# A dense product-key expert layer: 48 instead of 32 tokens of the last tile taken out of the dense stage, with rearranged PSUM, selection and tail

## The chip, the cores and the metric

The kernel runs on one core of one Trainium2 chip. The core has five engines with an instruction queue each: TensorE (PE in the profile, its weight loads PEld), VectorE (DVE), ScalarE (ACT), GpSimd (POOL) and SyncE (SP, which only issues DMAs here). They wait for each other by semaphores. The metric is the device time of one execution in microseconds (us), the median of several runs; smaller is better.

## The reference, cut to what matters

Two decoder layers over 512 tokens of width 1024. Each is a mixer (gated linear attention in the first, stick-breaking attention in the second, both with memory attention), a residual with layer norm, and then a PEER layer: every token picks 8 x 16 of 16384 experts, and each expert is one row of a table `u` and one row of a table `v`.

```python
def peer(x, w_q, subkeys, u_tab, v_tab):
    ...
    q = (xf @ w_q).reshape(N, PEER_HEADS, 2, PEER_QHALF)
    s = jnp.einsum('nhpd,hpkd->nhpk', q, subkeys).astype(jnp.float32)
    top_s, top_i = lax.top_k(s, PEER_TOPK)
    ...
    best_s, best_pos = lax.top_k(cand_s, PEER_TOPK)
    idx = jnp.take_along_axis(cand_i, best_pos, axis=-1)
    g = jax.nn.softmax(best_s, axis=-1).astype(x.dtype)
    ...
        act = jax.nn.gelu(jnp.einsum('nd,nhkd->nhk', xt, u_tab[it]), approximate=False)
        return jnp.einsum('nhk,nhkd->nd', gt * act, v_tab[it])
```

All data are 32-bit. The products run as three matmuls on a split of both operands into a high and a low part (`hi*hi`, `hi*lo`, `lo*hi`).

## The kernel before

The 512 tokens are four tiles of 128. All four are treated alike up to the selection of experts; then the work of `peer` (line 1122 on) is divided in three ways.

- **Tile 0 is gathered.** For each of its 128 (head, k) places one indirect DMA from POOL fetches 128 rows of `u` (512 KB, tile `gr`), and DVE multiplies them with x and sums up (`gather_u`, tile `gh`); later the same is done with rows of `v`, added up with weights in `va` (`gather_v`).
- **Tiles 1 to 3 are dense**: the hidden values of all 16384 experts are computed in 128 blocks of 128 experts. A block (`ublock`) loads a block of `u` (SP, `ur`), splits it (`uh` on ACT, `ul` = `ur` - `uh` on DVE or POOL), makes 24 matmuls into a PSUM tile `ph` (8 chunks of the width by 3 products, lines 118 to 120), and ACT applies the Gelu and writes the result out to memory (`act`, tensor `Ad`; the last 16 blocks stay in SBUF as `keep`).
- **Side tokens**: the last `SD` = 32 of tile 3 are left out of these matmuls, so that a matmul moves `TU` = 384 - 32 = 352 columns. Their hidden values come from gathered rows of `u`, 16 tokens in a group: 8 heads x 16 tokens fill the 128 partitions, and 16 gathers make a group. Indices, weights and results change their layout by small trips through memory (`Si`, `Sg`, `Sw`), issued by SP. Their x stands in an SBUF tile `xr`, copied eight times by eight DMAs of SP (`side_x`, line 1170).

The gate of each dense or side token at each expert is spread out by one-hot matmuls (`pg`: two per dense token in `gate_mm`, three per side token in `side_mm`), evicted by ACT and written to memory (`Gd`, 24 groups of 16 tokens). Then follows the v stage, 128 blocks again: `vprep` loads a block of `v` (`vr`) and of the activations (`al`) and gates (`gl`), multiplies the two (`w`), splits both (`vh`, `vl`, `whi`, `wlo`), and 18 matmuls of 512 columns (`mov_mm`, lines 290 to 294) add into six PSUM tiles `acc`. The last `TAIL` = 6 blocks are held back and run tile by tile at the end, so that one tile's layer norm (`finish`) can run beside the next tile's matmuls.

The order on PE, DVE, ACT and POOL is written out by hand (`manual_schedule`). In the u stage each block has a place for other work: a small planner (constants `BLK`, `GU`, `GUA`, `GUM` and so on) gives every block a number of nanoseconds for gathers, selection and gates. `later` holds splits `ul` that have not been given to an engine; `topk16` gives one to POOL whole, a gather of tile 0 gives half to DVE and half to POOL, and `flush` gives what is left to DVE. The selection of three tiles is made while their queries are computed, the fourth's during the u stage.

PSUM has eight banks of 512 columns. During the u stage six of them rotate under one tag `ps`, for `ph`, `pg` and the small transposes alike, and two hold x of tile 0 (`xs`).

Of the kernel before, what the change touches and what calls it, by code (L numbers as in the profile page):

```python
# [64 lines left out]
@contextmanager  # L65
def psum_pool(E, **tags):

    with E.tc.tile_pool(name="ps", bufs=1, space=bass.MemoryType.PSUM, reuse_waits="tile") as p:
        E.ps, old = (p, tags), getattr(E, "ps", None)
        yield  # L70
        E.ps = old


def psum(E, name="ps", tag="ps"):
    p, tags = E.ps
    if tag == "xs":
# [923 lines left out]
def x_to_T(E, t, tag="ps"):  # L1000

    nc = E.nc
    both = psum(E, name="xtp", tag=tag) if tag == "xs" else None
    for g in range(2):
        ps = both[:, g * 512:(g + 1) * 512] if tag == "xs" else psum(E, name="xtp", tag=tag)
# [64 lines left out]
SG = 2  # L1070
SD = SG * TS
TU = TD - SD
ST = NT - 1
S0 = P - SD
NSUB = TD // TS
# [19 lines left out]
WF = 6800  # L1095
ER = 16
# [28 lines left out]
def peer(E, mixer, wq, sk, ut, vt, un, lng, lnb, out_dram=None, follow=()):  # L1125
# [11 lines left out]
    with ExitStack() as pp:  # L1137
# [74 lines left out]

        def flush():
# [3 lines left out]
        def gather_u():  # L1217
# [48 lines left out]
        def gather_v():  # L1266
# [11 lines left out]
            finish(0, [va[:, :512], va[:, 512:]])  # L1278
            yield 4000
# [4 lines left out]
        with ExitStack() as up:  # L1284
# [6 lines left out]
            def topk16(*jobs, pool=True):  # L1291

                done = later and pool
# [17 lines left out]
            class Sel:  # L1311

                def __init__(self, t):
                    self.t = t
                    self.top_s = wk.tile([P, 16, 16], F32, tag="top_s", name="top_s", bufs=3)
                    self.top_i = wk.tile([P, 16, 16], U32, tag="top_i", name="top_i", bufs=3)
# [3 lines left out]
                    self.nr = self.nc = 0  # L1320
# [13 lines left out]
                def stage2(self):  # L1334
# [5 lines left out]
                    for a, n, o, w in SEG:  # L1340
                        dst = cand[:, :, o:o + n * w].rearrange("p h (a w) -> p h a w", a=n)
                        V.tensor_add(dst, v[:, 0, :, a:a + n, None].to_broadcast([P, 4, n, w]),
                                     v[:, 1, :, None, 0:w].to_broadcast([P, 4, n, w]))
                    for q in range(0, 4, 2):
                        jobs = []
                        for k in range(q, q + 2):
                            c2 = wk.tile([P, 64], F32, tag="s2", name="c2")
# [672 lines left out]
```

## Time and profile before

| | us |
|---|---|
| runs: median (3 runs, 2811.19 to 2813.94) | 2812.4 |
| profiled execution | 2810.38 |
| its span, first to last instruction | 2808.7 |
| u stage of layer 1 and of layer 2 (first to last `ph`) | 545.5 and 545.3 |
| v stage up to its tail (layer 1 and 2) | 497.6 and 497.6 |
| DVE busy over the span | 2325.0 (83%) |
| mean DMA rate over the span | 293 GB/s |

The profile names a group of instructions by line, engine, operation and tiles (written <- read). Its windows give the busy time of each engine in a stretch, then the granted TensorE clock (1.00 is full), the mean busy share of the 16 DMA engines and the rate in GB/s. A DMA share slightly above 1 is possible, since packets overlap. A matmul's own duration is modelled; its cadence is read from the count in a stretch.

### The profile page before, as it was taken

How to read it: one execution, taken by the hardware profiler on the slowest of the kernel's cores; microseconds unless marked ns; L12 is line 12 of the kernel's file. 1: busy time of each engine (PE TensorE's matmuls, PEld its weight loads, DVE VectorE, ACT ScalarE, POOL GpSimd, SP SyncE). 2: the span in 40 equal slices, each digit the busy share in tenths (PEclk: the TensorE clock that was granted, in tenths of full speed). 3: DMA queues.
4: the chain of work that ended last, by engine and by line, in shares of the span. 5: the costliest groups of instructions: out<-in, count | busy, mean ns of one | idle time of the engine just before them, and what ended most of it. 6: DMA issues, size and time to landing. Idle time of an engine off the chain costs nothing.

```text
span 2808.7 us, 45526 instructions
## 1 busy us (share of the span) xinstructions
PE 2789.2 (99%) x16235; PEld 2476.1 (88%) x16235; DVE 2325.0 (83%) x4816; ACT 1443.0 (51%) x2701; POOL 1141.3 (41%) x839
## 2 busy tenths in 40 slices
PE   9999999999999999999999999999999999999998
PEld 8888899999999888888787889999999988888886
DVE  5565999998766898888868859999987768888888
ACT  6342458576864443434346534585868544334432
POOL 0102564665664344444100025636656733343440
PEclk9999999999999999999999999999999999999999
DMA  5332499999999999999621325999999999999994
GB/s 195 117 113 76 160 321 369 329 372 334 365 356 385 345 390 380 380 383 386 209 68 46 120 84 182 319 367 333 367 346 360 359 374 363 386 370 382 385 382 156
DMA packets 277556, 822.37 MB, mean 293 GB/s; under 512 B 36976, under 2 KB 86352, under 8 KB 270928
## 3 DMA queue, kind: packets, MB, share of 16 engines
q1 hardware_dynamic: 170336, 423.42, 41.8%
q0 software_dynamic: 83264, 303.08, 29.3%
q10 hardware_dynamic: 23728, 92.96, 8.3%
q8 instruction: 127, 2.08, 0.3%
q14 instruction: 101, 0.83, 0.1%
HBM read 723.83 MB, written 93.42 MB: 291 GB/s over the span
## 4 chain that ended last, share of the span: by engine, by line
PE 91%; DVE 6%; DMA 1%; issue 1%; ACT 0%; POOL 0%; DVEq 0%; SPq 0%; ACTq 0%; POOLq 0%
PE acc L290 12%; PE acc L294 12%; PE acc L292 12%; PE ph L118 10%; PE ph L120 10%; PE ph L119 10%; PE pq L118 2%; PE pq L119 2%; PE pq L120 2%; DVE gr L1120 1%; PE pg L1637 1%; PE pg L1638 1%; PE pss L1709 1%; PE bsp L118 1%; PE oacc L290 1%; PE oacc L294 1%
## 5 line engine op out<-in xcount | busy, mean ns | idle before, releaser
L118 PE MATMUL ph<-xhl,uh 128*128 128x352 f32 x2048 | 674.2, 329 | 0.0
L99 POOL TENSOR_TENSOR ul<-ur,uh 128x512 fp32r<-128x512 f32 (+1 forms) x222 | 382.5, 1723 | 691.3 <-DVE s L1302 366.6
L120 PE MATMUL ph<-xhl,ul 128*128 128x352 f32 x2048 | 661.0, 323 | 1.2 <-POOL ul L99 1.2
L119 PE MATMUL ph<-xhl,uh 128*128 128x352 f32 x2048 | 660.6, 323 | 0.0
L1181 POOL DMA_INDIRECT gr<-in_vt,gidx x256 | 349.1, 1364 | 482.7 <-DVE va L1274 437.9
L98 ACT ACTIVATE vh<-vr 128x1024 fp32r<-128x1024 f32 x248 | 262.7, 1059 | 431.6 <-PE acc L294 279.9
L290 PE MATMUL acc<-vh,whi 128*128 128x512 f32 x1480 | 456.1, 389 | 1.4 <-ACT whi L1863 1.4
L292 PE MATMUL acc<-vl,whi 128*128 128x512 f32 x1480 | 455.7, 389 | 0.0
L294 PE MATMUL acc<-vh,wlo 128*128 128x512 f32 x1480 | 455.7, 389 | 0.0
L98 ACT ACTIVATE uh<-ur 128x1024 fp32r<-128x1024 f32 x288 | 303.5, 1054 | 219.4 <-PE ph L119 67.0
L99 DVE TENSOR_TENSOR vl<-vr,vh 128x1024 fp32r<-128x1024 f32 x248 | 303.3, 1223 | 122.6 <-ACT vh L98 116.9
L120 PEld LDWEIGHTS ph<-xhl,ul 128*128 128x128 f32 x2048 | 385.1, 188 | 2.4 <-POOL ul L99 2.4
L119 PEld LDWEIGHTS ph<-xhl,uh 128*128 128x128 f32 x2048 | 385.7, 188 | 0.0
L118 PEld LDWEIGHTS ph<-xhl,uh 128*128 128x128 f32 x2048 | 385.4, 188 | 0.1
L1181 POOL DMA_INDIRECT gr<-in_un,gidx x256 | 298.3, 1165 | 163.7 <-DVE gr L1120 114.9
L290 PEld LDWEIGHTS acc<-vh,whi 128*128 128x128 f32 x1480 | 277.4, 188 | 60.4 <-ACT whi L1863 3.1
L292 PEld LDWEIGHTS acc<-vl,whi 128*128 128x128 f32 x1480 | 277.5, 188 | 58.2 <-DVE vl L99 0.8
L294 PEld LDWEIGHTS acc<-vh,wlo 128*128 128x128 f32 x1480 | 277.5, 188 | 58.0 <-DVE wlo L1864 0.7
L1274 DVE SCALAR_TENSOR_TENSOR va<-gr,gw,va 128x1024 f32<-128x1024 f32 x254 | 324.8, 1279 | 1.8
L1120 DVE SCALAR_TENSOR_TENSOR gr<-gr,x 128x1024 f32<-128x1024 f32 x250 | 300.4, 1213 | 0.9 <-DMA gr<-in_un,gidx 0.7
L1617 ACT ACTIVATE obl<-ob,rat 128x128 f16<-128x128 f16 x704 | 223.9, 392 | 40.8 <-DVE ob L1120 23.0
L1120 DVE TENSOR_TENSOR ul<-ur,uh 128x512 fp32r<-128x512 f32 (+1 forms) x230 | 190.0, 828 | 62.1 <-ACT uh L98 61.0
(390 smaller groups left out, 4498.3 us busy)
## 6 DMA issues: line engine op xcount, KB each, us to landing
ur<-in_ut SPq DMA_DIRECT2D x256, 512.0 KB
vr<-in_vt SPq DMA_DIRECT2D x256, 512.0 KB
Gd<-gt ACTq DMA_DIRECT2D x48, 1024.0 KB
Ad<-act ACTq DMA_DIRECT2D x112, 352.0 KB
al<-Ad SPq DMA_DIRECT2D x112, 352.0 KB
gl<-Gd SPq DMA_DIRECT2D x144, 256.0 KB
ur<-in_wq SPq DMA_DIRECT2D x32, 512.0 KB
bs<-in_b_st SPq DMA_DIRECT2D x14, 512.0 KB
```

The costliest lines, as they stand in the source:

```text
L98: nc.scalar.activation(hi, raw, AF.Copy)
L99: sub = lambda eng=eng, sl=slice(None): eng.tensor_sub(lo[:, sl], raw[:, sl], hi[:, sl].bitcast(F32))
L118: nc.tensor.matmul(ps, h, xhi[:, c, sl], start=(c == 0), stop=False)
L119: nc.tensor.matmul(ps, h, xlo[:, c, sl], start=False, stop=False)
L120: nc.tensor.matmul(ps, l, xhi[:, c, sl], start=False, stop=(c == NC - 1))
L290: nc.tensor.matmul(acc[hf], lh, hi[:, hf * 512:(hf + 1) * 512], start=first, stop=False)
L292: nc.tensor.matmul(acc[hf], lh, lo[:, hf * 512:(hf + 1) * 512], start=False, stop=False)
L294: nc.tensor.matmul(acc[hf], ll, hi[:, hf * 512:(hf + 1) * 512], start=False, stop=last)
L1120: self.ins = op(*args, **kw)
L1181: nc.gpsimd.indirect_dma_start(out=gr, out_offset=None, in_=tab, in_offset=bass.IndirectOffsetOnAxis(ap=idx[:, k:k + 1], axis=0))
L1274: nc.vector.scalar_tensor_tensor(va, gr, gw[:, k:k + 1], va, op0=ALU.mult, op1=ALU.add)
L1617: nc.scalar.activation(obl[:, q], ob[:, q, 0], AF.Copy, scale=rat[:, n0 + q:n0 + q + 1])
```

## The change

- `SG` goes from 2 to 3 groups of side tokens, `SD` from 32 to 48, `TU` from 352 to 336 columns. 16 more gathers of `u` per layer, one more group of small trips, and a third `side_gates`.
- The u stage's PSUM is divided by tag: two banks for `ph`, two for `pg` and the transposes, two (`xr`) for the side group's x. ACT copies `xr` into the latter (`side_psum`); the next group's `xr` is loaded earlier.
- With x in PSUM, a side gather now also hands half of a pending `ul` to DVE and half to POOL, where it gave the whole to DVE before.
- Eight of the sixteen rows of the fourth tile are selected during the queries (`ER` 8; the tile's results stand in place of tile 0's finished scores in `sall`).
- The transposed gates leave PSUM by ACT (list `soon`), no longer by DVE.
- The planner's constants change (`BLK`, `GUA`, `GUX`, `GUZ`, `GUM`, `WF`).
- At the v stage's end the last blocks are prepared two per block, so that all are issued by block 121; tile 0's layer norm comes behind them, and the transposes of its result stand among the second tile's matmuls.

```diff
-        E.ps, old = (p, tags), getattr(E, "ps", None)
+        old = getattr(E, "ps", None)
+        E.ps = p, tags, old
...
-SG = 2
+SG = 3
...
-GU, GUA, GUX, GUZ, GUM = 800, 1450, 1400, 1300, 2400
+GU, GUA, GUX, GUZ, GUM = 800, 1700, 1550, 1350, 3000
...
-BLK, SUM, LOW, HOT, REST = 4050, 450, 1150, 1900, 1.12
+BLK, SUM, LOW, HOT, REST = 3650, 450, 1150, 1900, 1.12
...
-WF = 6800
-ER = 16
+WF = 6200
+ER = 8
...
+        def side_psum(xr):
+            x = psum(E, name="sx", tag="xr")
+            nc.scalar.activation(x, xr, AF.Copy)
+            return x
...
-                if xr is not None:
-                    flush()
-                else:
-                    xr = xnat[-1]
-                    if later and len(xnat) > 1:
-                        did["half"] += 1
-                        low, was = later.pop(0), V.ins
-                        low(V, slice(0, LW))
-                        after(E, low(nc.gpsimd, slice(LW, D)), was)
+                xr = xnat[-1] if xr is None else xr
+                if later and len(xnat) > 1:
+                    did["half"] += 1
+                    low, was = later.pop(0), V.ins
+                    low(V, slice(0, LW))
+                    after(E, low(nc.gpsimd, slice(LW, D)), was)
...
+                        side["next"] = side_x(side["g"] + 1)
...
-            finish(0, [va[:, :512], va[:, 512:]])
-            yield 4000
+            vp["va"] = va
...
-                on = [sel for sel in sels if row < ER or sel is not sels[2]]
-                topk16(*[sel.job() for sel in on[:2]])
-                if on[2:]:
-                    topk16(on[2].job())
+                on = sels if row < ER else sels[:3]
+                for k in range(0, len(on), 2):
+                    topk16(*[sel.job() for sel in on[k:k + 2]])
...
-            pp.enter_context(psum_pool(E, ps=6, xs=1))
+            pp.enter_context(psum_pool(E, xs=1))
...
+            ups = ExitStack()
+            ups.enter_context(psum_pool(E, ph=2, pg=2, xr=1))
...
-                    pn = psum(E, name="ph")
+                    pn = psum(E, name="ph", tag="ph")
...
+                while soon:
+                    soon.pop(0)()
...
+            at = 2
             for b in range(P):
-                vprep(b + 2)
+                while at <= b + 2 + max(0, b + 4 + TAIL - P):
+                    vprep(at)
+                    at += 1
...
             gus.drain()
+            finish(0, [vp["va"][:, :512], vp["va"][:, 512:]])
...
+                        if t == 1 and k == TAIL // 2 and not last:
+                            x_to_T(E, 0, ("ps", "xs"))
```

Three places show how instructions move.

**PE, u stage of layer 1, first matmuls of block 41** (`ph` is the block's PSUM tile, `uh`, `ul` its split weights; in brackets the engine on which a row waits). Before:

```order
L120 MATMUL ph<-xhl,ul 128x352
L118 MATMUL ph<-xhl,uh 128x352 [waits Activation_49]
L119 MATMUL ph<-xhl,uh 128x352
L120 MATMUL ph<-xhl,ul 128x352 [waits DVE_49]
L118 MATMUL ph<-xhl,uh 128x352
```

With the change:

```order
L123 MATMUL ph<-xhl,ul 128x336
L121 MATMUL ph<-xhl,uh 128x336 [waits Activation_49]
L122 MATMUL ph<-xhl,uh 128x336
L123 MATMUL ph<-xhl,ul 128x336 [waits DVE_49]
L121 MATMUL ph<-xhl,uh 128x336
```

The rows differ in the columns, 336 for 352. The wait on ACT is another one: before, it is for `uh` of this block, and `ph` has one of six banks; with the change it is for the Gelu of the block before last, which reads the bank that this block writes. Of 128 first matmuls of a block in layer 1, 57 carry a wait on ACT before, 103 with the change.

**POOL, u stage of layer 1, the first side group** (`gr<-in_un,si` are side gathers, `ul` the splits that POOL gets). Before:

```order
L1181 DMA gr<-in_un,si 128x1024
L99 TENSOR_TENSOR ul<-ur,uh 128x512
L1181 DMA gr<-in_un,si 128x1024 x13
L99 TENSOR_TENSOR ul<-ur,uh 128x1024
L1181 DMA gr<-in_un,si 128x1024
```

With the change:

```order
L1185 DMA gr<-in_un,si 128x1024
L102 TENSOR_TENSOR ul<-ur,uh 128x512
L1185 DMA gr<-in_un,si 128x1024 x2
L102 TENSOR_TENSOR ul<-ur,uh 128x512
L1185 DMA gr<-in_un,si 128x1024
```

Where 13 gathers of a group followed each other on POOL, halves of `ul` now stand between them. Over the whole program POOL's halves go from 172 to 220, DVE's from 172 to 220, DVE's whole ones from 66 to 16. Of a layer's gathers 143 stood ahead of the last `ul` on POOL and 145 behind it; now 150 and 154.

**DVE, end of the v stage of layer 1** (`w`, `vtail`, `wlo` prepare a held-back block; `va` is the last gather's sum, `lny<-xnat,va` the start of tile 0's layer norm). Before:

```order
L1274 SCALAR_TENSOR_TENSOR va<-gr,gw,va 128x1024
L1028 SCALAR_TENSOR_TENSOR lny<-xnat,va 128x512
L1030 BN_STATS lnst<-lny 128x6
...
L1045 SCALAR_TENSOR_TENSOR xnat<-lny,lnsm,bet 128x512 x2
L1852 TENSOR_TENSOR w<-gl,al 128x352
L99 TENSOR_TENSOR vtail<-vr,vtail 128x1024
L1864 TENSOR_TENSOR wlo<-w,whi 128x384
```

With the change:

```order
L1281 SCALAR_TENSOR_TENSOR va<-gr,gw,va 128x1024
L1880 TENSOR_TENSOR w<-gl,al 128x336
L102 TENSOR_TENSOR vl<-vr,vh 128x1024
L1892 TENSOR_TENSOR wlo<-w,whi 128x384
L1880 TENSOR_TENSOR w<-gl,al 128x336
L102 TENSOR_TENSOR vtail<-vr,vtail 128x1024
L1892 TENSOR_TENSOR wlo<-w,whi 128x384
...
L1030 SCALAR_TENSOR_TENSOR lny<-xnat,va 128x512
```

Before, the layer norm of tile 0 stood between the last gather and all six held-back blocks; now it stands behind them.

More of the change, by code (lines that the diff above doesn't have):

```diff
@@ L74, in psum @@
 def psum(E, name="ps", tag="ps"):
-    p, tags = E.ps
-    if tag == "xs":
+    p, tags, out = E.ps
+    while tag not in tags:
+        p, tags, out = out
+    if tag in ("xs", "xr"):
         return p.tile([P, D], F32, tag=tag, name=name, bufs=tags[tag])
@@ L1002, in x_to_T @@
     nc = E.nc
-    both = psum(E, name="xtp", tag=tag) if tag == "xs" else None
     for g in range(2):
-        ps = both[:, g * 512:(g + 1) * 512] if tag == "xs" else psum(E, name="xtp", tag=tag)
+        ps = psum(E, name="xtp", tag=tag if isinstance(tag, str) else tag[g])[:, :512]
         for j in range(4):
@@ L1073 @@
 ST = NT - 1
+TA = 352
 S0 = P - SD
+SA = S0 // 32 * 32
 NSUB = TD // TS
@@ L1289, in peer, with topk16 @@
             did.update(low=0, half=0, hot=0, sum=0)
-            def topk16(*jobs, pool=True):
-                done = later and pool
+            def topk16(*jobs):
+                done = len(later)
                 if done:
@@ L1311, in peer, with __init__, open @@
             class Sel:
-                def __init__(self, t):
+                def __init__(self, t, over=None):
                     self.t = t
-                    self.top_s = wk.tile([P, 16, 16], F32, tag="top_s", name="top_s", bufs=3)
-                    self.top_i = wk.tile([P, 16, 16], U32, tag="top_i", name="top_i", bufs=3)
+                    self.nr = self.nc = 0
+                    if over is not None:
+                        self.top_s, self.top_i = sall[:, :, over, 0:16], sall.bitcast(U32)[:, :, over, 16:32]
+                    else:
+                        self.top_s = wk.tile([P, 16, 16], F32, tag="top_s", name="top_s", bufs=3)
+                        self.top_i = wk.tile([P, 16, 16], U32, tag="top_i", name="top_i", bufs=3)
+                        self.open()
+                def open(self):
                     self.best = wk.tile([P, 8, 16], F32, tag="best", name="best", bufs=3)
@@ L1343, in stage2 @@
                                      v[:, 1, :, None, 0:w].to_broadcast([P, 4, n, w]))
+                    jobs = []
                     for q in range(0, 4, 2):
-                        jobs = []
-                        for k in range(q, q + 2):
-                            c2 = wk.tile([P, 64], F32, tag="s2", name="c2")
-                            jobs.append((self.best[:, h + k], self.pos[:, h + k], cand[:, k], c2))
-                        topk16(*jobs, pool=False)
-                        yield 2300 if q == 0 else 1700
+                        c2 = wk.tile([P, 2, 64], F32, tag="s2", name="c2")
+                        for k in range(2):
+                            jobs.append((self.best[:, h + q + k], self.pos[:, h + q + k], cand[:, q + k], c2[:, k]))
+                    yield 4000 - topk16(*jobs)
                 def rows(self):
@@ L1497, in side_load @@
                     yield
-                side.update(left=TS, g=0, sh=sh[:, 0], sg=sg, all=sh, x=xr0[0], idx=si[:, 0], si=si)
+                side.update(left=TS, g=0, sh=sh[:, 0], sg=sg, all=sh, x=side_psum(xr0[0]), idx=si[:, 0], si=si)
             def side_next():
                 g = side["g"] + 1
-                side.update(left=TS, g=g, sh=side["all"][:, g], x=side_x(g), idx=side["si"][:, g])
+                side.update(left=TS, g=g, sh=side["all"][:, g], x=side_psum(side["next"]), idx=side["si"][:, g])
             def side_late(g, sh):
@@ L1647, in peer @@
             avail = [0]
-            sels = [Sel(t) for t in order[:3]]
+            sels = [Sel(t) for t in order[:3]] + [Sel(order[3], order[0])]
             first = sels[0] if gat else None
@@ L1662, in rest @@
                         continue
-                    sel = sels[k] if k < 3 else Sel(t)
+                    sel = sels[k]
+                    if k == 3:
+                        sel.open()
                     rows = sel.rows()
@@ L1755, in ublock @@
                     if (b - 1) % AB == 0:
-                        ab = wk.tile([P, AB, TU], F32, tag="act", name="act")
+                        ab = wk.tile([P, AB * TA], F32, tag="act", name="act")[:, :AB * TU].rearrange("p (a n) -> p a n", n=TU)
                 pn = None
@@ L1779, in ublock @@
                 if b < P - 1:
-                    room += HALF * len(later) * (not side["left"])
+                    room += HALF * len(later)
                     gus(min(max(room, GU), GUA if work.q else GUX if b < BG else GUZ), GUM)
```

54 lines of the change are left out of this document (34 added, 20 removed).

## The prediction

> **What bounds the kernel now.** I began with the page's busy shares and its chain of waits, because they say whether any engine but one matters.
>
> ```profile
> span 2808.7 us, 45526 instructions
> PE 2789.2 (99%) x16235; PEld 2476.1 (88%) x16235; DVE 2325.0 (83%) x4816; ACT 1443.0 (51%) x2701; POOL 1141.3 (41%) x839
> PE 91%; DVE 6%; DMA 1%; issue 1%; ACT 0%; POOL 0%; DVEq 0%; SPq 0%; ACTq 0%; POOLq 0%
> ```
>
> PE is busy for 2789 of 2809 us: fewer PE cycles are worth their full time, as long as nothing else becomes late. So I read PE's waits next.
>
> ```profile
> PE xtp L1008 <- DVE xhl L1013: 3.3, 1, 3.3
> PE acc L290 <- ACT whi L1863: 2.7, 8, 0.3
> PE ph L120 <- POOL ul L99: 1.2, 3, 0.5
> ```
>
> (Total, times, longest.) The two big loops hardly wait; the first two rows are their tails. Then the windows by stage: u stage, v stage and tail of layer 1, then the same of layer 2.
>
> ```profile
> core 0: us, PE busy (x) PEld busy (x) DVE busy (x) ACT busy (x) POOL busy (x), PEclk, DMA share, GB/s
> 330.90:876.40 545.50, 544.75 (x3887) 533.44 (x3886) 467.08 (x1119) 363.49 (x742) 330.46 (x237) 1.00 0.94 348
> 876.40:1374.00 497.60, 497.60 (x2196) 411.99 (x2196) 436.31 (x544) 202.27 (x372) 194.20 (x145) 1.00 0.99 368
> 1374.00:1385.30 11.30, 9.93 (x38) 5.55 (x36) 11.29 (x18) 9.05 (x16) 0.00 (x0) 1.00 0.71 220
> 1385.30:1389.60 4.30, 1.01 (x9) 0.77 (x8) 3.77 (x6) 1.84 (x3) 0.00 (x0) 1.00 0.82 278
> 1389.60:1393.10 3.50, 3.50 (x11) 2.80 (x10) 2.45 (x5) 0.80 (x2) 0.00 (x0) 0.51 0.00 1
> 1729.60:2274.90 545.30, 544.81 (x3887) 533.48 (x3886) 466.58 (x1119) 363.46 (x742) 330.56 (x237) 1.00 0.95 348
> 2274.90:2772.50 497.60, 497.60 (x2197) 412.00 (x2196) 436.98 (x544) 202.08 (x372) 183.67 (x142) 1.00 0.98 368
> 2772.40:2783.70 11.30, 9.93 (x38) 5.63 (x37) 10.72 (x17) 7.51 (x14) 0.00 (x0) 1.00 0.30 95
> ```
>
> In both loops PE never stops, yet the DMA share is 0.94 to 0.99. PE is the bound and the DMA engines stand right behind it: a faster PE asks more of them per us.
>
> **A. Columns, 352 to 336.** A matmul's duration is modelled, so I take cadences: a stretch of blocks without gates (matmuls of `ph` alone), and one of the v stage.
>
> ```profile
> 497.55:528.25 30.70, 30.70 (x194) 30.70 (x193) 3.59 (x8) 1.00 0.99 356
> 1006.80:1072.10 65.30, 65.30 (x290) 54.06 (x289) 57.67 (x69) 26.29 (x48) 27.12 (x20) 1.00 1.02 387
> ```
>
> Eight blocks have 192 matmuls: 30.70 / 192 = 160.0 ns at 352 columns. Sixteen v blocks have 288: 226.7 ns at 512. So a column is worth 66.7 / 160 = 0.417 ns, and 16 columns 6.67 ns. Two layers x 128 blocks x 24 = 6144 matmuls: **-41.0 us**. A fixed part of the time would show as a smaller slope between the two cadences; 160.0 / 352 = 0.454 shows that there is one (about 13 ns), and the slope leaves it out. The v stage's matmuls don't shrink: tokens are their stationary side.
>
> **B. Gates.** A u stage lasts 545.5 us, of which 128 x 3.84 = 491.5 are `ph`; the other 54.0 belong to its 800 gate matmuls, 67 ns each. A side token takes three instead of two, so 16 more per layer: **+2.1**.
>
> **C. Tails.** Six blocks at 6 x 0.2267 us each are 8.16 us, and took 11.3 in either layer: 3.1 lost, because `w` and `vtail` of these blocks stood behind tile 0's layer norm on DVE. Prepared by block 121, they should not be waited for. Layer 1 further loses 3.3 us on `xtp` (tile 0's transposes, which now stand among the second tile's matmuls), and 1.7 after it: the clock was 0.51 for 3.5 us. Together 6.2 + 3.3 + 1.7 = 11.2. Bounds -5 (the second tile's weights or tile 0's layer norm come late again) and -11; I take **-10**.
>
> **D. Two banks for `ph`.** A block may now start only when the Gelu of the block before last has ended. In the trace of before that order often would not hold, because ACT serves its splits in turn, and those wait for `u`.
>
> ```profile
> ACT uh L98 <- DMA ur<-in_ut: 29.1, 13, 4.5
> ACT uh L98 <- DMA ur<-in_ut: 25.9, 12, 4.6
> ```
>
> (Layer 1, then layer 2.) The deepest place, on ACT and on SP:
>
> ```profile
> 513.98 1.06 ACT L98 ACTIVATE uh<-ur 128x1024 fp32r<-128x1024 f32 x1 [4.51 <-DMA ur<-in_ut]
> 514.94 0.44 ACT L1767 ACTIVATE act<-ph 128x352 f32<-128x352 f32 x1
> ...
> 508.28 0.42 SPq L1515 DMA_DIRECT2D Sw<-sh  x1
> 510.69 0.33 SPq L83 DMA_DIRECT2D ur<-in_ut  x1
> 520.19 0.33 SPq L1519 DMA_DIRECT2D sw<-Sw  x1
> ```
>
> That Gelu is block 42's and ends at 515.4, while block 44 starts at 497.55 + 4 x 3.84 = 512.9. With six banks PE runs on; with two it would stand for 2.5 us, with the Gelu behind the late split. Behind a block's first matmul stand all its others, and behind those the next Gelu, so the time is lost and not caught up. SP is part of the cause: the trip of the side results holds it between the last two rows, and a third group means a third trip. Laid over all blocks in this way, some eight places of a layer would be late, by 0.3 to 2.6 us each. Bounds: nothing (the loads come sooner in the new order) to 10 per layer (the 29 us of ACT's waits, less the 1 to 2 us that a Gelu has to spare at each of 13 places). Waits overlap, since a stalled PE lets the loads catch up: 4.5 per layer, **+9**. The two banks for gates are evicted in 0.6 us and seldom queue; I put them into the same bounds.
>
> **E. Traffic in the v stage.** A gather moves 303.08 MB / 576 = 0.526 MB:
>
> ```profile
> q0 software_dynamic: 83264, 303.08, 29.3%
> Ad<-act ACTq DMA_DIRECT2D x112, 352.0 KB
> al<-Ad SPq DMA_DIRECT2D x112, 352.0 KB
> ```
>
> By the order on POOL 154 instead of 145 gathers of a layer run behind the u stage: +4.7 MB, less 16 columns of `al` (-0.9): +3.8 on 497.6 x 0.368 = 183 MB. On the mean that needs 376 GB/s, in the stage's middle, which runs at 387, about 395. What such stretches reached, and how near the edge they were:
>
> ```profile
> 1024.00:1040.00 16.00, 16.00 (x72) 13.23 (x72) 12.38 (x15) 6.83 (x13) 5.80 (x5) 1.00 1.03 402
> 752.00:768.00 16.00, 16.00 (x132) 15.48 (x131) 12.32 (x17) 13.41 (x34) 10.41 (x8) 1.00 1.02 413
> 1267.90:1333.20 65.30, 65.30 (x289) 54.05 (x288) 57.34 (x69) 26.19 (x48) 30.65 (x20) 1.00 1.01 384
> ...
> 1295.38 1.22 DVE L99 TENSOR_TENSOR vl<-vr,vh 128x1024 fp32r<-128x1024 f32 x1
> ...
> 1296.94 0.62 PE L292 MATMUL acc<-vl,whi 128*128 128x512 f32 x2
> ```
>
> `vl` was ready at 1296.6, 0.35 us before its matmul. So the middle cannot take all of it unseen. Bounds 0 and 3.8 / 0.384 = 9.9 us per layer; I take 2.5 per layer, **+5**, near the lower end because stretches of 16 us did reach 402.
>
> **F. Traffic in the u stage.** Seven more gathers (3.7 MB) and 16 loads of `xr` (0.5), less `Ad` (0.9): 189.8 + 3.3 = 193.1 MB, in about 526 us: 367 GB/s, what the v stage moves today without a stall. **0**, and more than that only as the third rival.
>
> **G. Selection in the queries.**
>
> ```profile
> L1300 DVE MAX8 top_s<-sall 128x8 f32<-128x128 f32 x42 | 10.6, 279 | 16.6 <-ACT sall L1710 16.6
> 246.00:330.90 84.90, 84.90 (x437) 72.32 (x436) 69.73 (x440) 32.44 (x46) 39.36 (x20) 1.00 0.34 114
> ```
>
> A row's selection is five instructions of about this length (0.25 to 0.29 us) and three short loads, about 1.56 us, so eight rows add 12.5 us; by the order on DVE about half of that leaves the stage with other work. DVE has 84.9 - 69.7 = 15.2 us idle under PE: **0**, or 3 to 6 per layer if these rows end the stage.
>
> **H. DVE and POOL in the u stage.**
>
> ```profile
> L1120 DVE TENSOR_TENSOR ul<-ur,uh 128x512 fp32r<-128x512 f32 x86 | 59.9, 697 | 29.8 <-ACT uh L98 29.6
> L1120 DVE TENSOR_TENSOR ul<-ur,uh 128x1024 fp32r<-128x1024 f32 x29 | 35.3, 1216 | 0.5 <-ACT uh L98 0.5
> L1120 DVE SCALAR_TENSOR_TENSOR gr<-gr,x 128x1024 f32<-128x1024 f32 x106 | 127.5, 1213 | 0.9 <-DMA gr<-in_un,gidx 0.7 <-issue 0.2
> L99 POOL TENSOR_TENSOR ul<-ur,uh 128x512 fp32r<-128x512 f32 x86 | 131.1, 1525 | 124.1 <-DVE ob L1120 35.5 <-PE ph L120 19.7 <-ACT uh L98 19.6
> ```
>
> DVE per layer: 24 halves more (+16.7), 25 whole ones fewer (-30.4), seven products more (+8.5), some 6 net of selection gone: about 456 of 526 us. POOL: 24 halves (+36.6) and seven issues (+8): 375 of 526. Both lie under PE: **0**. In the v stage DVE comes to 436 + 9 x 1.28 = 448 of 497.6.
>
> Sum: -41.0 + 2.1 - 10 + 9 + 5 = -34.9, against the profiled execution of 2810.4: 2775.5. The median of the runs is 2.0 above it, so I forecast **2778 us**.
>
> **Rivals.**
>
> - **Nothing stalls** (D and E cost nothing): 2812.4 - 41.0 + 2.1 - 11 = 2763. For it: PE waits today only in the tails. Against: block 42's Gelu and `vl`'s 0.35 us. Chance 0.15.
> - **The two banks cost the upper bound**, or the tails give only 5 with D somewhat higher: 2778 + 11 = 2789. For it: a shorter block leaves each load less time. Chance 0.18.
> - **Today's rates are the ceiling, and it comes out slower.** If the DMA engines move no more than 348 GB/s in the u stage's mixture and 368 in the v stage's, the stages last 193.1 / 0.348 = 555 and 186.9 / 0.368 = 508 us: +9.5 and +10.3 per layer, with -10 of the tails +29.6: 2842. It becomes slower than before where the u stage stays below 352 GB/s (548 us, with C and E as above). For it: the DMA share of 0.94 to 0.99, and loads that ACT already waits for. Against it, from the u stage itself:
>
> ```profile
> 739.90:812.50 72.60, 72.60 (x569) 70.64 (x566) 57.07 (x81) 59.20 (x140) 48.20 (x37) 1.00 0.99 376
> 845.50:876.40 30.90, 30.90 (x195) 30.90 (x194) 15.75 (x26) 11.10 (x18) 20.27 (x16) 1.00 1.05 387
> ```
>
>   Its own stretches reach 376 and 387, so the mean of 348 is demand, not a ceiling. Chance 0.08.
> - **The change doesn't do what it says at the tail**: `whi` has few buffers, so a block prepared early may wait for one that PE still reads; then C gives the 5 us of `xtp` and clock alone, 2783. Chance 0.09, which lies inside the forecast's surroundings.
>
> The Trainium skill, page "DMA: Bandwidth & Descriptors", section "Specifications", gives a limit of about 358 GB/s between HBM and one core, under a fabric ceiling of 435. An estimate by 358 would make the u stage 539 us and the v stage 522, and the time about 2839, as the third rival has it. This trace disagrees: 368 GB/s over 497.6 us and 387 over 65 lie above that limit, and so the rule adds nothing to that rival's chance.
>
> **How the numbers follow.** The forecast itself (2770 to 2784) has 0.47, the four rivals 0.50, and 0.03 stays for a ceiling that binds in part and leaves the time as it was. About 0.2% (5.6 us) is what a measurement of this kernel can tell from no change. Slower is the third rival's 0.08; the same (2807 to 2818) the 0.03; faster 0.89. The range reaches from the first rival to a little above the second, 2762 to 2798; what is left out is mostly the ceiling.
>
> **What would show it.** A: the cadence of gate-free blocks falls to 153.3 ns; anything else and the slope is wrong. C: no wait at `xtp`, six tail blocks in 8.2 to 9 us, no slice with a clock of 0.5. D: a new row in PE's waits, `ph` <- ACT `act`, about 4.5 us per layer; absent, the loads come sooner; above 10, the second rival. E: PE waits for `vl` or `vh` in the v stage's middle, 2.5 us per layer, at 385 to 400 GB/s. F: a u stage of 525 to 532 us at about 365 GB/s; one of 545 or more at 350 with waits for `uh` at every block would be the third rival, and the forecast wrong. G: the query stage unchanged at 84.9 us.

## The result and the profile after

The changed kernel takes 2798.14 us (median of five runs, 2791.01 to 2802.96) against 2812.26 for the kernel before: a ratio of 0.9948, interval 0.9938 to 0.9959. It is faster, as forecast, but by 14 us and not by 34; the forecast was 2778, the range ended at 2798.0. The profiled execution was the slowest of the five, 2802.96.

Its page, the same three rows as of before:

```profile
span 2801.2 us, 45941 instructions
PE 2762.1 (99%) x16269; PEld 2442.1 (87%) x16269; DVE 2333.6 (83%) x4910; ACT 1443.4 (52%) x2689; POOL 1253.1 (45%) x923
PE 74%; DVE 12%; DMA 8%; issue 3%; ACT 2%; POOL 0%; SPq 0%; ACTq 0%; DVEq 0%; POOLq 0%
```

PE's busy time fell by 27 us, the span by 7.5. The chain of waits, 91% PE before, now runs 12% over DVE and 8% over DMAs. PE's waits (total, times, longest) show where:

```profile
PE ph L123 <- DVE ul L1124: 6.7, 4, 1.8
PE ph L121 <- ACT act L1793: 5.5, 5, 1.8
PE pg L1594 <- DVE ob L1124: 5.4, 4, 1.6
PE ph L123 <- POOL ul L102: 1.9, 4, 0.7
PE acc L293 <- ACT whi L1891: 1.7, 4, 0.7
PE pg L1660 <- DVE ob L1124: 1.4, 2, 0.7
PE xtp L1010 <- DVE xhl L1015: 1.2, 1, 1.2
PE pg L1660 <- ACT gt L1664: 0.8, 2, 0.4
```

Before, the rows for `ph` and `pg` came to 1.2 us. A row counts the idle time from the modelled end of the last matmul; counted from start to start, each wait is longer (the first one below, 1.67 us in its row, costs 1.84). The windows: u stage, v stage and six tail blocks of layer 1, u and v stage of layer 2, then eight blocks without gates, and two short stretches.

```profile
core 0: us, PE busy (x) PEld busy (x) DVE busy (x) ACT busy (x) POOL busy (x), PEclk, DMA share, GB/s
330.30:874.50 544.20, 532.56 (x3904) 518.52 (x3903) 461.99 (x1126) 363.00 (x739) 372.73 (x275) 0.99 0.96 358
874.30:1374.80 500.50, 499.55 (x2199) 411.30 (x2198) 444.38 (x560) 209.20 (x381) 206.95 (x154) 1.00 1.01 378
1374.80:1383.00 8.20, 8.20 (x38) 6.79 (x37) 7.96 (x16) 3.71 (x6) 0.00 (x0) 1.00 0.53 177
1723.40:2264.20 540.80, 529.86 (x3904) 516.83 (x3903) 461.94 (x1124) 362.44 (x737) 370.74 (x275) 1.00 0.96 359
2264.00:2768.00 504.00, 502.08 (x2198) 410.26 (x2198) 445.44 (x561) 209.36 (x383) 211.74 (x151) 1.00 1.00 374
500.10:529.80 29.70, 29.70 (x197) 29.68 (x195) 26.19 (x95) 17.31 (x23) 24.02 (x18) 1.00 1.02 367
354.60:358.00 3.40, 3.40 (x14) 3.40 (x14) 3.19 (x12) 0.00 (x0) 2.07 (x3) 0.50 0.59 186
839.30:842.70 3.40, 3.40 (x18) 3.40 (x16) 0.48 (x1) 1.99 (x3) 0.44 (x1) 0.50 1.05 424
```

The u stages were forecast at about 526 us before waits and took 544.2 and 540.8. The v stages lost 2.6 and 6.1 (from the first matmul to the first of the tail, 497.8 us before). The tail's six blocks take 8.2 us, as forecast. The last two rows show half a clock for 3.4 us each, behind clusters of waits; a third such stretch lies at 1747.2. Each costs 1.7 us of PE work.

The first cluster is at the start of the u stage. DVE, POOL and PE there, and the pair of waits ahead of the second half-clock stretch:

```profile
339.63 1.22 DVE L1124 SCALAR_TENSOR_TENSOR gr<-gr,x 128x1024 f32<-128x1024 f32 x1 [1.16 <-DMA gr<-in_un,gidx]
342.88 0.69 DVE L1124 TENSOR_TENSOR ul<-ur,uh 128x512 fp32r<-128x512 f32 x1
346.22 2.52 DVE L1124 TENSOR_TENSOR cand<-top_s 128x64 f32<-128x64 f32 x4
...
345.83 2.40 POOL L102 TENSOR_TENSOR ul<-ur,uh 128x1024 fp32r<-128x1024 f32 x1
...
343.62 0.42 PE L123 MATMUL ph<-xhl,ul 128*128 128x336 f32 x1 [1.67 <-DVE ul L1124]
354.01 0.42 PE L123 MATMUL ph<-xhl,ul 128*128 128x336 f32 x1 [1.77 <-DVE ul L1124]
...
836.78 0.23 PE L1594 MATMUL pg<-ob 128*128 128x128 bf16 x1 [1.30 <-DVE ob L1124]
...
838.88 0.23 PE L1594 MATMUL pg<-ob 128*128 128x128 bf16 x1 [1.26 <-DVE ob L1124]
```

DVE waits for gathered rows that were asked for late, with `ul` behind them: POOL starts the first gather of `u` at 334.7 us, 4.4 into the u stage, where before it started at 317.7, 13 us ahead of it. Then the four `cand` sums, 0.61 us together when nothing is beside them, take 2.52 beside POOL's split. This clash is not new: before, two of the six groups of `cand` in the u stage of layer 1 begin with a sum of 2.3 and 1.4 us instead of 0.2, but PE did not wait behind them. The second pair of waits, for `ob`, stands where the last side group's gates are emptied out together.

### The profile page after: what moved, and what is told of

Its sections match the earlier page's. It is cut to its first block, busy times and chain, and to the rows that moved or that the text cites. A ratio compares the mean times of both kernels' runs of the same rounds, so it can differ in the third digit from the quotient of the medians.

```text
span 2801.2 us, 45941 instructions
## 1 busy us (share of the span) xinstructions
PE 2762.1 (99%) x16269; PEld 2442.1 (87%) x16269; DVE 2333.6 (83%) x4910; ACT 1443.4 (52%) x2689; POOL 1253.1 (45%) x923
## 4 chain that ended last, share of the span: by engine, by line
PE 74%; DVE 12%; DMA 8%; issue 3%; ACT 2%; POOL 0%; SPq 0%; ACTq 0%; DVEq 0%; POOLq 0%
PE ph L121 9%; PE ph L123 9%; PE ph L122 9%; PE acc L295 7%; PE acc L297 7%; PE acc L293 7%; DMA vr<-in_vt 5%; DVE va L1281 3%; PE pq L121 2%; PE pq L122 2%; PE pq L123 2%; DVE vl L102 2%; DVE wlo L1892 1%; DVE gr L1124 1%; PE pg L1661 1%
## 5 line engine op out<-in xcount | busy, mean ns | idle before, releaser
L121 PE MATMUL ph<-xhl,uh 128*128 128x336 f32 x2048 | 661.6, 323 | 5.6 <-ACT act L1793 5.5
L123 PE MATMUL ph<-xhl,ul 128*128 128x336 f32 x2048 | 649.5, 317 | 8.6 <-DVE ul L1124 6.7
L122 PE MATMUL ph<-xhl,uh 128*128 128x336 f32 x2048 | 648.1, 316 | 0.0
L102 POOL TENSOR_TENSOR ul<-ur,uh 128x512 fp32r<-128x512 f32 (+1 forms) x272 | 457.6, 1683 | 424.8 <-ACT uh L101 156.3
L1185 POOL DMA_INDIRECT gr<-in_vt,gidx x256 | 366.8, 1433 | 421.2 <-DVE va L1281 367.4
L1124 DVE SCALAR_TENSOR_TENSOR gr<-gr,x 128x1024 f32<-128x1024 f32 x256 | 307.6, 1214 | 13.7 <-DMA gr<-in_un,gidx 13.5
L1891 ACT ACTIVATE whi<-w 128x384 fp32r<-128x384 f32 x256 | 133.1, 520 | 230.2 <-DVE w L1880 229.4
L1640 ACT ACTIVATE obl<-ob,rat 128x128 f16<-128x128 f16 x672 | 213.6, 392 | 31.6 <-ACT gt L1664 13.8
```

Source lines behind the costliest of these rows:

```text
L102: sub = lambda eng=eng, sl=slice(None): eng.tensor_sub(lo[:, sl], raw[:, sl], hi[:, sl].bitcast(F32))
L121: nc.tensor.matmul(ps, h, xhi[:, c, sl], start=(c == 0), stop=False)
L122: nc.tensor.matmul(ps, h, xlo[:, c, sl], start=False, stop=False)
L123: nc.tensor.matmul(ps, l, xhi[:, c, sl], start=False, stop=(c == NC - 1))
L1124: self.ins = op(*args, **kw)
L1185: nc.gpsimd.indirect_dma_start(out=gr, out_offset=None, in_=tab, in_offset=bass.IndirectOffsetOnAxis(ap=idx[:, k:k + 1], axis=0))
```

## The experiments

All are compared by their ratio to the kernel before, which ran beside each group (medians 2811.7 to 2813.9). Where one version is said to differ from another by ratio, the difference of the two ratios is meant. A hunk says what was edited; `...` stands for what is left out of it.

### The controls: the tail alone, the change again, two groups

The kernel before with the tail's part of the diff alone:

> The kernel before with nothing changed but the end of the v stage (last blocks prepared two per block, tile 0's layer norm behind them, the transposes of its result among the second tile's matmuls). If the tail is worth what step C says: -8 to -11 us against before (2801 to 2804), six tail blocks in 8.2 to 9 us, the wait at xtp gone or under 1.5 us. If preparing earlier only moves the waiting into the v stage: 0 to -4 us, with new waits for whi or vl before block 122.

Measured 2804.54 us against 2813.13, ratio 0.9971 (0.9959 to 0.9983): -8.6 us. In its trace the tails take 29.1 and 24.5 us instead of 34.5 and 27.6, no half clock follows them, and the v stages stay at 498. The tail is a gain of its own.

> The changed kernel as it is, on the chip of the three runs beside it: what they are compared with. If the earlier difference of -14 us carries over, 2795 to 2803. If the chips differ in how fast their DMA engines deliver, the v stages (500.5 and 504.0 us in the first trace) are the part that moves.

Measured 2799.27 (2798.26 to 2800.32), 0.9949 (0.9936 to 0.9963): the difference carries over. In its trace the u stages take 539.2 and 541.7 us, the v stages 501.7 and 502.4. The waits for `ul` (6.9 us) and for `ob` of the last side gates (5.5) stand in the same places.

```diff
-SG = 3
+SG = 2
-            gst = Stream(..., side_gates(0), side_gates(1), gates(list(range(0, P, OT))), side_gates(2))
+            gst = Stream(..., side_gates(0), gates(list(range(0, P, OT))), side_gates(1))
```

> The changed kernel with two side groups (SG 3 to 2, and the third group's gates taken off the list): 352 columns, 16 gathers and products per layer less, all else as changed. If the third group's work is what brings the new waits of the u stage, those waits go, and the time is that of the new tail alone, 2802 to 2807: the columns' 41 us are then mostly lost to the work that pays for them. If the waits come from the new arrangement (two banks, order, selection) they stay at some 12 us per layer and the time is 2820 or more: the third group is then worth its 41 us.

Measured 2824.2, 1.0040 (1.0027 to 1.0053). (A first try, with the third group's gates still on the list, gave no time.)

```profile
331.00:888.90 557.90, 549.58 (x3887) 535.91 (x3886) 456.62 (x1108) 366.35 (x750) 370.84 (x275) 1.00 0.96 355
888.80:1386.80 498.00, 498.00 (x2198) 412.32 (x2197) 431.39 (x527) 206.12 (x383) 161.66 (x137) 1.00 0.98 359
```

With 352 columns the new arrangement's u stage takes 557.9 us, 12 more than before. So most of the waits come from the arrangement, not from the third group's work. By its rows they are 5.9 us for `ul` and 9.1 for the Gelu and its like on ACT (`act`, `keep`, `gt`), and none for `ob`: those come with the third group. The third group is worth 25 us (2824.2 to 2799.3), and the arrangement costs 20 (2824.2 against the tail alone, 2804.5). The v stage without the third group's work is back at 498.0: these 8 us for two layers are the larger part of what the group falls short of its 39 (41 less 2 for its gates).

### Volume: less DVE work, less traffic

```diff
-                V.scalar_tensor_tensor(gr, gr, 1.0, xr, ..., accum_out=dst[:, k:k + 1])
+                n = D if dst is gh else 512
+                V.scalar_tensor_tensor(gr[:, :n], gr[:, :n], 1.0, xr[:, :n], ..., accum_out=dst[:, k:k + 1])
```

> The changed kernel with the 48 products of the side gathers per layer over half of each row (512 of 1024 elements; the rows are still fetched whole, and the side tokens' hidden values are those of half rows). This takes 48 x 0.55 = 26 us of DVE work per layer out of the u stage, behind its first 30 us, and no traffic. Theory 3 (DVE sets when ul and ob are ready): the waits for ob and the Gelu in the middle and at the end of the u stage shrink, those at its first blocks, ahead of the side gathers, stay: -5 to -10 us against the changed kernel (2799). If the DMA engines set the pace of the u stage: 0 to -3 us.

Measured 2797.23 (2790.33 to 2807.21), 0.9959 (0.9946 to 0.9972): no gain that the intervals show, though 26 us of DVE work per layer were gone. The waits for `ul` (6.5 us) and `ob` (5.5) are unchanged.

```diff
-            nc.gpsimd.indirect_dma_start(out=gr, ..., in_=tab, ...)
+            n = D if idx is gidx else 512
+            nc.gpsimd.indirect_dma_start(out=gr[:, :n], ..., in_=tab if n == D else tab.rearrange("e (two d) -> (e two) d", two=2), ...)
...
+                    junk = gp.tile([P, D], F32, tag="va", name="va")
+                    V.scalar_tensor_tensor(two(junk), gr[:, None, :512].to_broadcast([P, 2, 512]), 1.0, two(xr), ..., accum_out=dst[:, k:k + 1])
```

> The changed kernel with half of each row fetched in the 48 side gathers per layer (2 KB for 4 KB, the products as long as before on the half row read twice; the hidden values of the side tokens are not those of their experts). This takes 48 x 0.25 = 12.6 MB per layer out of the u stage's 193 MB (6.5%), and no DVE work. If the DMA engines set the pace (the third rival, for the u stage): -8 to -14 us against the changed kernel (2799), most of it as shorter waits for the Gelu and at the u stage's end. Theory 3: 0 to -3 us, the waits for ul and ob stay as they are.

Measured 2811.66, 0.9998 (0.9987 to 1.0009): 14 us slower than the change, with 25 MB less. On ACT, SP and PE:

```profile
598.35 1.03 ACT L1220 ACTIVATE sx<-xr 128x1024 f32<-128x1024 f32 x1 [5.56 <-DMA xr<-xnat]
...
583.03 9.43 SPq L1174 DMA_DIRECT2D xr<-xnat  x8
...
600.74 0.65 PE L121 MATMUL ph<-xhl,uh 128*128 128x336 f32 x1 [3.81 <-ACT act L1799]
```

The copy of the next side group's x into PSUM stands on ACT ahead of the Gelu, and waits for eight small loads that SP issues over 9.4 us; with two banks PE waits behind. But these loads are late through the edit itself: its scratch tile `junk` has the tag of `xr` (`va`) and so its only buffer, and the loads start at 490.5 and 583.0 us, right behind the last product of the group before (490.0 and 582.6), where the change issued them from 426 and 513 on. So the 14 us don't tell what the traffic is worth. What the run does show: at 333 GB/s instead of 358, the waits for `ul` (6.0 us) and `ob` (6.7) stay about as they were, and a late load on SP reaches PE through ACT.

```diff
-                if k + PF < P:
+                if k + PF < P - 9:
```

> The changed kernel with nine gathers of v per layer left out (119 of 128 places, the last row used again, so tile 0's result is not the reference's): 4.7 MB per layer less in the v stage, the same DVE work. Step E (the added traffic of the v stage costs PE time): the v stages fall from 501 to 504 us to about 498, as before the change: -5 to -8 us against the changed kernel (2799). If the v stage's loss comes from DVE or ACT being late: less than 2 us.

Measured 2798.63, 0.9953 (0.9940 to 0.9965): the same time. Its v stages took 500.7 and 499.7, against 501.7 and 502.4. Leaving out the last nine gathers keeps the pace in the middle as it was, so this edit did not separate volume from pace. The number of gathers alone does not order the losses either. By trace, the v stages with 134 gathers lost nothing, and with 142 nothing before the change, but 1.8 and 2.8 us here; with 146 and 147 (versions below) they lost 0.2 to 3.2; with 150 and 151 mostly 1.6 to 6, but 0.1 to 0.5 in the version with the gates sooner. At the longest wait of either v stage of the change (0.7 us at 1227, 0.5 at 2489) the load of `v` is late: `whi` stands on ACT behind a split `vh` that had waited 5.5 and 4.6 us for its `vr`. That the pace of the traffic makes these loads late is likely and not shown.

### PSUM and the Gelu

```diff
-            x = psum(E, name="sx", tag="xr")
-            nc.scalar.activation(x, xr, AF.Copy)
-            return x
+            return xr
-            ups.enter_context(psum_pool(E, ph=2, pg=2, xr=1))
+            ups.enter_context(psum_pool(E, ph=3, pg=3))
```

> The changed kernel with the side tokens' x left in SBUF, and its two PSUM banks given to ph and pg, three each. Theory 2 (two banks are what the u stage pays for): the waits of ph for the Gelu (5.5 us) and of pg for its eviction (0.8) go, and those for ul at the start shrink too: -10 us or more against the changed kernel. Theory 1: the 6 us of Gelu and eviction waits go, the waits for ul and ob at the two ends stay: -4 to -7 us, less up to 2 for the products from SBUF, which took 1.31 in place of 1.21 us before.

Measured 2840.73, 1.0103 (1.0087 to 1.0118). The side products, of the changed kernel and then of this one:

```profile
L1124 DVE SCALAR_TENSOR_TENSOR gr<-gr,sx 128x1024 f32<-128x1024 f32 x96 | 115.4, 1213 | 4.1 <-DMA gr<-in_un,si 3.9
```

```profile
L1124 DVE SCALAR_TENSOR_TENSOR gr<-gr,xr 128x1024 f32<-128x1024 f32 x96 | 190.9, 2000 | 1.5 <-DMA gr<-in_un,si 1.5
```

With POOL's halves of `ul` beside them, the products took 2.00 us instead of 1.21, and waits for `ul` rose to 26 us. The expectation took 1.31 from the kernel before, in which POOL had few splits there. The Gelu waits went, but x in PSUM is worth far more than a third bank. The Trainium skill, page "SBUF — State Buffer", section "Who interferes with whom", says that a VectorE instruction with two SBUF inputs contends with a GpSimd instruction that reads SBUF, over a port interface that the two share, and that one with at most one SBUF input does not. These rows agree (2.00 us with both operands in SBUF, 1.21 with one in PSUM), as do the `cand` rows above.

```diff
-                    if b > 0:
-                        prep(b + 18, later)
                     hi, lo = parts.pop(16 + b)
...
                 ph = pn
+                if 0 < b < P:
+                    prep(b + 18, later)
```

> The changed kernel with the order of ACT turned in each block of the u stage: the Gelu of the last block stands ahead of the split uh of a later block, and no longer behind it. Theory 2 in the form of step D (with two banks PE waits because the Gelu queues behind a split that waits for its load): the waits of ph for the Gelu (5.5 us) fall below 1 us, -5 to -8 us with a half-clock stretch less. If the Gelu is late for another reason (the scaled copies obl and the evictions on ACT), the waits stay; if uh then comes late, they turn into waits for uh or ul of the same size.

Measured 2801.82, 0.9960 (0.9947 to 0.9974), not better than the change.

```profile
PE pg L1660 <- ACT gt L1664: 3.7, 5, 1.5
```

The waits of `ph` for the Gelu fell to nothing and came back as waits of `pg` for its eviction (0.8 us before the edit). So ACT's queue as a whole seems to be late there, and not only the Gelu's place in it.

### The start of the u stage

```diff
                 ph = pn
                 while soon:
                     soon.pop(0)()
+                if b < 6:
+                    flush()
```

> The changed kernel with one edit: in the first six blocks of the u stage, pending splits ul are given to DVE ahead of the block's selection and gathers, and not behind them. Theory 1 (ul is late there because of what stands ahead of it on DVE): the waits of 4.6 and 4.4 us for ul at the start of the two u stages go, and with them most half-clock stretches of 3.4 us behind them (1.7 us each): -8 to -13 us against the changed kernel, 2785 to 2790. Theory 2 (the two banks of ph hold PE, and the waits for ul are only where it shows): the waits move to ph behind the Gelu, less than 3 us won. Theory 3 (DVE has too much work in these blocks in whatever order): the waits move to blocks 6 to 12, less than 3 us won.

Measured 2812.34, 0.9996 (0.9987 to 1.0005), 13 us slower than the change by ratio. Per layer DVE got 12 splits whole instead of 4 (1.22 us each, where a half takes 0.69), and POOL 103 halves instead of 110. The waits for `ul` stayed at 7.6 us while those for `ob` rose to 11.7. Its runs have a mean clock of 0.992 to 0.995.

```diff
-WF = 6200
+WF = 7400
```

> The changed kernel with one constant (WF 6200 to 7400): in the query stage, tile 0's candidates and indices gidx are made sooner on DVE, so that the first gathers are issued before the u stage begins. Theory 4 (at the start of the u stage DVE waits 2.0 us for gathered rows that were asked for too late, with the splits ul queued behind): the waits for ul of 4.6 and 4.4 us shrink below 2 us each, with the half-clock stretches behind them: -5 to -10 us against the changed kernel. Theory 3 (DVE has too much work in the first blocks, whatever waits in it): the waits stay above 3 us each, or show at a later block, under 3 us won. In either case the query stage must not grow by more than 1 us, or the gain is eaten there.

Measured 2794.44, 0.9938 (0.9924 to 0.9951): 4.8 us better than the change beside it, 3 by ratio, with intervals that overlap. The query stage stays at 103.7 us, and the first gather starts at 314.8. DVE has no wait for gathered rows in the first 36 us (2.1 us in the change), and of the three waits for `ul` in the first 25 us of the u stage one is left. But a clash of the same kind came later:

```profile
400.83 2.60 DVE L1124 TENSOR_TENSOR cand<-top_s 128x64 f32<-128x64 f32 x4
...
400.48 2.43 POOL L102 TENSOR_TENSOR ul<-ur,uh 128x1024 fp32r<-128x1024 f32 x1
...
410.55 0.42 PE L123 MATMUL ph<-xhl,ul 128*128 128x336 f32 x1 [1.91 <-DVE ul L1124]
```

```diff
-ER = 8
+ER = 0
```

> The changed kernel without the selection of eight rows of the fourth tile in the query stage (ER 8 to 0, as before the change): some 12 us of DVE work per layer go back into the u stage. Theory 4: tile 0's indices come sooner, as in the wider step of the run beside this one, so the waits for ul at the start shrink; the returned 12 us show as new waits later in the u stage, 2 to 6 us per layer: between -4 and +6 us against the changed kernel. Theory 3 (DVE is what the first half of the u stage waits for): slower by 8 to 15 us.

Measured 2802.17, 0.9954 (0.9940 to 0.9968), the change's time within the intervals.

```profile
PE pg L1594 <- DVE ob L1124: 10.3, 4, 3.9
PE ph L123 <- DVE ul L1124: 3.5, 4, 1.6
```

The waits for `ul` halve: the early rows are a part of the late start. The first gather starts at 329.7 us, 5 sooner than in the change and still 12 later than before the change, when `WF` was 6800 and not 6200. But the returned work makes the gates later, and their waits about double.

```diff
-                    return 1200 * len(jobs) - topk16(*jobs)
+                    return 1200 * len(jobs) - topk16(*jobs, pool=self.nr < 2 * self.nc + 8)
```

(`topk16` hands no split to POOL where `pool` is false.)

> The changed kernel; a row of the fourth tile's selection in the u stage no longer hands a whole split ul to POOL where DVE's next step is the sums cand of that tile. Theory 5: POOL's split of 2.4 us holds up DVE's cand beside it (2.5 us in place of 0.6), and the waits of PE right behind (1.94 us for ul at 352, 0.9 for ob at 414) are its price, so they go, with some half-clock stretches: -3 to -7 us against the changed kernel (2799). If the split that DVE gets instead (1.2 us) costs as much as the clash: within 2 us of it.

Measured 2809.32, 0.9990 (0.9981 to 0.9999): 11 us slower than the change. The `cand` sums are down to 0.61 us, but POOL gets its split later, and PE waits 2.2 us for that one. On POOL:

```profile
347.34 2.35 POOL L102 TENSOR_TENSOR ul<-ur,uh 128x1024 fp32r<-128x1024 f32 x1 [1.54 <-PE ph L123]
```

The gates shift too (waits for `ob` 11.7 us), and the clock is 0.993 to 0.996.

### The end of the u stage

```diff
-GR2 = 1.5
+GR2 = 1.8
```

> The changed kernel with one constant (GR2 1.5 to 1.8): from block 80 on a block takes more steps of the gates, so that the last side group's gates end at block 116 and are not emptied out together behind block 118. Theory 1 (the steps left over stand back to back on DVE and PE): the waits of 2.9 and 3.2 us for ob at the end of the u stages go, with a half-clock stretch behind them: -5 to -8 us against the changed kernel. Theory 3 (DVE is full there): ob stays late, less than 2 us won.

Measured 2809.01, 0.9989 (0.9980 to 0.9998): 11 us slower.

```profile
PE ph L121 <- ACT keep L1791: 8.4, 4, 3.5
...
PE pg L1594 <- DVE ob L1124: 2.3, 2, 1.1
```

The waits for `ob` shrank as meant; the last blocks, now sooner, wait for their Gelu (`keep`) behind splits whose loads stand on SP among the loads of gates and activations for the v stage. With 1.6 in place of 1.8:

> The changed kernel with the one constant GR2 1.5 to 1.6. If the waits for ob at the end of the two u stages (2.8 to 3.3 us each) and the half-clock stretches behind them are a cost of their own: 2789 to 2794, clock 0.998 or more in every run. If it moves other places into waits, as GR2 1.8 did: 2797 or more.

Measured 2797.43 (2795.93 to 2800.25), 0.9944 (0.9930 to 0.9957): the change's time. The last waits for `ob` fell to a single one of 0.7 us; those for `ul` stayed (7.8 us), and one for `keep` (1.2) came.

### Together

> The run before this one together with the sooner indices (WF 7400), which gave 2794 alone. Theory 4 and 5 as two causes of the start: about 1.7 us of waits for ul per layer are left at the start, and the time is 2786 to 2792. If the two edits take away the same wait: 2792 to 2796.

Sooner indices and no clash: 2791.35, 0.9924 (0.9912 to 0.9936).

> The second of these runs with the gates a little sooner (GR2 1.5 to 1.6), so that fewer steps of the last side group's gates are emitted back to back behind block 118. If the waits for ob there (2.8 to 3.3 us per layer) were a cost of their own: -4 to -6 us against the second run, 2782 to 2788. If the last blocks of the u stage would wait for their loads in any case, as in the run with GR2 1.8: no more than 2 us better, new waits of ph for keep.

And the gates at 1.6: 2783.79 (2782.23 to 2784.83), 0.9898 (0.9884 to 0.9913), the fastest version, 29 us under the kernel before and, by ratio, 14 under the change. Its waits and its four stages:

```profile
PE ph L121 <- ACT act L1793: 3.9, 5, 1.6
PE ph L123 <- DVE ul L1124: 3.0, 2, 1.5
PE gts L1542 <- ACT gt L1664: 2.8, 2, 1.4
PE ph L121 <- ACT keep L1791: 2.1, 2, 1.3
...
PE pg L1594 <- DVE ob L1124: 1.3, 2, 0.9
```

```profile
331.10:867.80 536.70, 528.84 (x3904) 515.21 (x3903) 462.19 (x1102) 362.65 (x738) 362.58 (x269) 1.00 0.97 360
867.70:1366.00 498.30, 498.30 (x2199) 412.27 (x2198) 439.02 (x551) 208.68 (x378) 201.23 (x150) 1.00 1.00 377
1717.10:2251.50 534.40, 528.24 (x3904) 515.23 (x3903) 462.18 (x1100) 362.77 (x738) 362.51 (x269) 1.00 0.97 362
2251.30:2749.80 498.50, 498.50 (x2200) 412.17 (x2199) 439.70 (x552) 208.52 (x378) 203.36 (x147) 1.00 1.00 375
```

No u stage has a slice at half clock (one stands in layer 1's tail). DVE and POOL are about as busy per stage as in the change (462 us, and 363 where it was 371 to 373): mainly the order moved. Against the repeated run of the change the two u stages together win 10 us and the v stages 8; the tails lose 3. So about half of the gain lies in the v stages, which lose 0.2 and 0.4 us here, with 147 gathers for 151; the sooner indices let some run ahead.

> The fastest version so far (2784) without its edit to POOL's splits: sooner indices (WF 7400) and gates a little sooner (GR2 1.6). If the edit to POOL's splits is worth the 3 us by which the second step of the last four runs beat the sooner indices alone: 2785 to 2789. If the last constant needs it (places shift, and another wait takes over): 2790 or more. If it was never needed: 2782 to 2785.

Without the edit to POOL's splits: 2799.85, 0.9949 (0.9936 to 0.9963), 14 us slower than with it by ratio. The `cand` groups over the u stage of layer 1, without and with:

```profile
L1124 DVE TENSOR_TENSOR cand<-top_s 128x64 f32<-128x64 f32 x8 | 3.7, 465 | 0.0
```

```profile
L1124 DVE TENSOR_TENSOR cand<-top_s 128x64 f32<-128x64 f32 x8 | 1.8, 220 | 0.0
```

Without it the waits for `ul` at 410 and 1802 us (1.9 and 3.1 us) are back. So the clash is a cause; but 14 us is more than its waits, and the same edit alone lost 11; why is not shown. The three edits hang together and do not add up.

## Why the prediction was right or wrong

- **A, right.** Where nothing waits, matmuls of `ph` follow at 153.4 ns (a mean without the outer tenths), forecast 153.3; eight whole blocks, with three small transposes among them, give 29.70 / 192 = 154.7.
- **B, right.** Counted from start to start, against the median step of each kind, the u stages lose 15.9 and 14.1 us at waits and 3.2 and 1.6 at half clock. What is left is 525 us each, 19.2 less than before; A and B have 19.4.
- **C, right.** -6.7 and -3.1 us by the tails of the traces, forecast -10; alone it measured -8.6. A wait of 1.2 us at `xtp` is left.
- **D, size about right, reason wrong.** Forecast 9 us, found 5.5 for the Gelu and 0.8 for the gates' eviction by the rows, 8.3 together from start to start. ACT's waits for `ur` in the u stage of layer 1 are 9.8 us in the repeated run, not 29; the Gelu stands behind the scaled copies `obl`, an eviction and the copies `tb`.
- **E, mis-sized.** Forecast 5, found 8.7 (8.3 in the repeated run), at 374 to 378 GB/s. The late loads are there as it has them, though PE's longest waits were for `whi` and not for `vl`. What sets their cost is open: the fastest version moves 375 to 377 GB/s and loses 0.6 in the two layers together.
- **F, right for what it claims.** The u stages ran at 358 GB/s, and the fastest version moves the same blocks in 536.7 and 534.4 us, at 360 and 362: this rate was not their bound. The 526 us that F assumed for a stage failed by the waits of H. (One more group is 8 loads of `xr`, not 16; the 0.5 MB is right.) What it left out is that the last blocks' loads queue on SP among the v stage's, as the run with the gates sooner showed.
- **G, right.** The query stage is unchanged at 103.7 us from its first matmul on. The early rows had their price behind it, at the start of the u stage.
- **H, the step that failed.** "Both lie under PE: 0." The busy times were nearly exact: 462 us on DVE against 456 forecast, 373 on POOL against 375. The cost was not in them: 8.6 us of waits for `ul`, 6.8 for `ob`, and three half-clock stretches (5.1). The working summed durations over a stage with 70 us to spare, and a queue served in order is late at places, not on the mean. Halving the side products changed nothing; moving instructions at almost the same busy times won 10 us in the u stages. Three such places stood in the order beforehand: tile 0's indices made later (first gather 17 us later), POOL's whole split beside `cand`, and the last side group's gates emptied out behind block 118.
- **The sum.** Against the forecast of 2775.5 for the profiled execution, 27.5 us are missing. From start to start, the waits for `ul` cost 8.0 more than before, those for `ob` 7.8, short ones for `obl` 3.5, the half clock 4.8, and the v stage 3.7 more than forecast; the Gelu and the evictions cost 0.7 less than D. Together 27.1.
- **The rivals.** Two banks at their upper bound (2789) would have come nearer in time, 9 us below, for the wrong reason. The ceiling of 348 GB/s is refuted; a ceiling near 375 in the v stage is not shown: the same rate was run with and without loss. That the tail's blocks are not really sooner is refuted.

## What to carry to other kernels

Where PE is back to back, price a moved or added instruction by what stands behind it in its queue at that place, not by the engine's total: here 26 us less work per layer on DVE won nothing, and short waits in one place cost more than they lasted, by the half clock behind them. Removing one wait shows the next one; edits to a hand-made order are to be tried together, since each alone may lose. And read the granted clock of every run: here a spread of 12 us between runs of one kernel, at clocks of 0.996 to 0.999, went with clusters of short waits.

## What the runs showed of the hardware

- **Half clock behind short waits.** Waits of 1.7, 0.7 and 1.8 us within 12 us were followed by 3.4 us at half clock in the profiled run of the change, and not in layer 1 of the repeated one; two of 1.3 us within 4 us had it as well. The Trainium skill, page "TensorE: Matmul & The Clock Gate", section "Part 1: The HAM clock gate (the "warmup" mystery)", speaks of an idle window of about 3.4 us that runs free of the program. The length of the stretch and its coming and going agree; that no single wait of the change was longer than 2 us does not fit a whole idle window.
- **The spread between runs is in part this clock.** Five runs of the change had 2791.0 and 2795.4 us at a mean clock of 0.999, 2798 to 2803 at 0.996 to 0.997. One thousandth of the clock is 2 x 0.001 x 2800 = 5.6 us at half speed, 2.8 us lost. The fastest version has 0.999 in each run and a spread of 2.6 us. But the clock is not all of it: the run with half products had 2790.3 and 2807.2 us, both at 0.999.
- **A small instruction can wait for a large one elsewhere.** Four sums of 0.61 us together took 2.5 us beside POOL's split, and products of two SBUF operands 2.0 on the mean instead of 1.2.
